# One decoder layer in fp32: the scheduler that orders each engine's instructions is given its other simulator

## The chip, the cores and the metric

The kernel runs on one core of one Trainium2 chip. The metric is the device time of one execution in microseconds (us); lower is better. Work is spread over TensorE (PE, matrix products; PEld is its weight load), VectorE (DVE), ScalarE (ACT), GpSimd (POOL) and the DMA queues, most of which are fed by SyncE (SP).

## What is computed

One layer of a hybrid decoder on 512 tokens of width 1024, all in fp32. The reference, cut to its frame:

```python
h = h + 0.5 * rmsnorm(swiglu(rmsnorm(h, ffn1_pre_w), ffn1_w_gu, ffn1_w_down), ffn1_post_w)
u = rmsnorm(h, mix_pre_w)
proj = u @ w_in                                    # 1024 x 10240, split into the branches' parts
y = gate0 * (hgrn2(...) @ w_br_hg) + gate1 * (dilated_attention(...) @ w_br_dil) \
  + gate2 * (memory_attention(...) @ w_br_mem)
h = h + rmsnorm(y @ w_out, mix_post_w)
h = h + 0.5 * rmsnorm(swiglu(rmsnorm(h, ffn2_pre_w), ffn2_w_gu, ffn2_w_down), ffn2_post_w)
```

`hgrn2` is a gated linear recurrence in chunks of 64 tokens, `dilated_attention` a sliding-window attention in three groups whose softmax statistics are merged, `memory_attention` a cross-attention into 256 memory tokens. `ffn1` and `ffn2` have 2816 hidden columns.

## The kernel before

**Products.** Every fp32 weight block is split into a high and a low part (`split`, L161 on ACT for the high part, L158 on DVE for the low part: lo = src - hi), so that three passes of a fast matmul replace one slow one: `mm3` (L341 to L343) for plain products, `product` (L361 to L363) for the Strassen-like products of `pair`, which computes two 128-row outputs from seven half-width products. The split parts live in a pool of 18 buffers named `w`; the raw weights arrive in 4 buffers `st`, 2 buffers `sh`, and 5 buffers `sum`. Where a pair needs sums of weight blocks, POOL starts DMAs that add while they copy (L303) or DVE adds (`sum<-...`). Activations stand in SBUF as `xhi`/`xlo` and `t1` to `t4`; PSUM has 5 buffers `ps` for the large products and 3 buffers `px` for everything smaller. A pool of 37 buffers `s` holds all other values.

**Stages.** FFN 1 runs to about 370 us, token mixing to about 1005 us, FFN 2 to the end. The seams between them are chains that go tile by tile (four tiles of 128 tokens): squares on ACT (L174), `rstd` with a sum on DVE (L180) and a power on POOL (L181), a scaling on DVE (L244 for the norm after a stage, L190 for the norm ahead of the next), transposes on PE (L352, `px<-ident,s`), and the split of the result (`xhi` on ACT, `xlo` on DVE). In token mixing, side tasks (HGRN heads, attention heads) issue small matmuls (L348, `px<-s,s`) between the large projections. A dilated head also exchanges its softmax statistics through DRAM: `x<-st` and then `ot<-x`, both DMAs of POOL's queue (L764 to L769), after which DVE merges them (`mm<-st,ot`).

**What sets the order.** Two things do. The source emits instructions in one sequence: a planner in the source (`spawn`, `tick`, the delays in `LAT`) decides where in the stream of large matmuls a side task's next step is emitted. This part is fixed text. Then the tile framework, when its context closes, runs a list scheduler: it plays the program on a simulated machine, and whenever a simulated engine is free it issues to it, of the instructions whose inputs and buffers are ready in the simulation, the one that stands first in the source's sequence. The order in which the simulated engine took them is the order in which the real engine gets them, and buffers of a pool are given out in that order too. The chip then runs each engine's list strictly from front to back, each instruction waiting on semaphores for its inputs. So an instruction that the simulation held ready too early stands too early in its list, and on the chip everything behind it on that engine waits with it.

**What is not free to move.** DMAs of `fetch` (L141) keep the source's order on SP; weight loads of `bring` (L151) may move among themselves behind an anchor. In the first stretch (`strict`, until FFN 1's first products start) `pin` also keeps splits, squares and DVE's two-operand work in the source's order.

## Time and profile before

| what | us |
|---|---|
| time, median of 3 runs (1366.94 to 1368.05) | 1367.82 |
| the profiled execution's own time | 1367.62 |
| its span, first to last instruction | 1365.8 |
| PE busy | 1331.6 |
| DVE busy | 1050.7 |
| ACT busy | 742.2 |
| POOL busy | 107.0 |

The granted TensorE clock was 0.998 of full speed on average over the span. Busy time of PE contains the pipelined tail of each matmul, so the idle time before an instruction is a little shorter than the time for which no matmul started. In views of the order of time a row gives the start, the length, the engine, the line, what is written from what, how many instructions were merged, and in brackets the idle time of that engine just before and what ended it.

### The profile page before, as it was taken

The numbers are of one execution on the slowest core, as the hardware profiler recorded it, in microseconds if no ns is written. First come the engines' busy times: TensorE is split into PE (matmuls) and PEld (weight loads), VectorE is DVE, ScalarE is ACT, GpSimd is POOL, SyncE is SP. The second block draws the span as 40 slices with busy tenths as digits, with TensorE's granted clock in tenths as the row PEclk, the third lists the DMA queues.
The fourth block names the chain that finished last, engine by engine and source line by source line (L and its number), as shares of the span: only waits on it lengthen the run. The fifth ranks groups of instructions, "written<-read, shape, count | busy, mean of one in ns | idle before, by whom it ended". The sixth has DMA issues, their size and how long they took to land.

```text
span 1365.8 us, 24324 instructions
## 1 busy us (share of the span) xinstructions
PE 1331.6 (97%) x9197; PEld 1233.0 (90%) x9197; DVE 1050.7 (77%) x1996; ACT 742.2 (54%) x1527; POOL 107.0 (8%) x140
## 2 busy tenths in 40 slices
PE   6999999999999999999999999999999999999997
PEld 6999999999789888899899999999889999999996
DVE  6887776777798975598888988897478877677765
ACT  6665544555467655355554755566366655445541
POOL 1111111110100000000000100000011111111100
PEclk9999999999999999999999999999999999999999
DMA  9676565554435335334224333335465765655513
GB/s 271 141 182 184 148 156 142 143 151 125 168 94 177 96 98 163 123 102 117 63 78 124 100 95 93 108 94 154 135 190 135 186 181 151 152 139 148 146 47 139
DMA packets 238123, 185.76 MB, mean 136 GB/s; under 512 B 9109, under 2 KB 198966, under 8 KB 238006
## 3 DMA queue, kind: packets, MB, share of 16 engines
q1 hardware_dynamic: 224246, 160.02, 39.5%
q0 software_dynamic: 12032, 21.04, 9.4%
q10 hardware_dynamic: 1728, 3.15, 0.6%
q8 instruction: 72, 1.18, 0.3%
q14 instruction: 45, 0.37, 0.1%
HBM read 153.73 MB, written 9.47 MB: 119 GB/s over the span
## 4 chain that ended last, share of the span: by engine, by line
PE 87%; DVE 6%; issue 3%; DMA 2%; ACT 1%; POOL 1%; SPq 0%; POOLq 0%; DVEq 0%; ACTq 0%
PE ps L361 17%; PE ps L363 17%; PE ps L362 17%; PE ps L341 6%; PE ps L342 6%; PE ps L343 6%; PE px L341 5%; PE px L342 5%; PE px L343 5%; PE px L348 4%; DVE s L158 2%; PE px L352 1%; DVE w L158 1%; POOL r L181 1%; DVE s L244 1%
## 5 line engine op out<-in xcount | busy, mean ns | idle before, releaser
L161 ACT ACTIVATE w<-sum 128x512 fp32r<-128x512 f32 x288 | 180.2, 631 | 215.9 <-PE ps L362 180.3
L158 DVE TENSOR_TENSOR w<-sum,w 128x512 fp32r<-128x512 f32 x288 | 196.9, 687 | 76.9 <-ACT w L161 75.9
L361 PE MATMUL ps<-xhi,w 128*128 128x256 f32 x864 | 246.3, 285 | 0.9 <-ACT s L379 0.9
L363 PE MATMUL ps<-xhi,w 128*128 128x256 f32 x864 | 244.8, 283 | 0.0
L362 PE MATMUL ps<-xlo,w 128*128 128x256 f32 x864 | 244.4, 283 | 0.0
L161 ACT ACTIVATE w<-st 128x512 fp32r<-128x512 f32 x260 | 162.9, 630 | 126.7 <-PE ps L362 90.0
L158 DVE TENSOR_TENSOR w<-st,w 128x512 fp32r<-128x512 f32 x260 | 177.2, 688 | 39.3 <-ACT w L161 37.9
L158 DVE TENSOR_TENSOR s<-s,s 128x256 f32<-128x256 f32 (+3 forms) x316 | 176.8, 564 | 16.2 <-ACT s L161 4.6
L361 PEld LDWEIGHTS ps<-xhi,w 128*128 128x128 f32 x864 | 165.6, 192 | 3.8 <-ACT s L379 1.2
L362 PEld LDWEIGHTS ps<-xlo,w 128*128 128x128 f32 x864 | 165.6, 192 | 2.4 <-issue 0.2
L363 PEld LDWEIGHTS ps<-xhi,w 128*128 128x128 f32 x864 | 165.5, 192 | 0.0
L158 DVE TENSOR_TENSOR sum<-sum,st 128x512 f32<-128x512 f32 x176 | 120.4, 687 | 10.9 <-issue 5.0
L158 DVE TENSOR_TENSOR s<-s,ps 128x256 f32<-128x256 f32 (+1 forms) x194 | 92.3, 476 | 29.4 <-PE ps L343 24.0
L341 PE MATMUL px<-s,s 128*128 128x512 f32 x288 | 112.6, 391 | 0.0
L342 PE MATMUL px<-s,s 128*128 128x512 f32 x288 | 112.5, 391 | 0.0
L343 PE MATMUL px<-s,s 128*128 128x512 f32 x288 | 112.0, 389 | 0.0
L361 PE MATMUL ps<-t4hi,w 128*128 128x256 f32 x288 | 81.9, 284 | 0.8 <-ACT s L382 0.8
L361 PE MATMUL ps<-t3hi,w 128*128 128x256 f32 x288 | 82.6, 287 | 0.0
L362 PE MATMUL ps<-t3lo,w 128*128 128x256 f32 x288 | 82.0, 285 | 0.0
L361 PE MATMUL ps<-t1hi,w 128*128 128x256 f32 x288 | 81.7, 284 | 0.0
L363 PE MATMUL ps<-t1hi,w 128*128 128x256 f32 x288 | 81.6, 283 | 0.0
L362 PE MATMUL ps<-t2lo,w 128*128 128x256 f32 x288 | 81.5, 283 | 0.0
(186 smaller groups left out, 3344.2 us busy)
## 6 DMA issues: line engine op xcount, KB each, us to landing
st<-in_ffn_w_gu_dram SPq DMA_DIRECT2D x48, 512.0 KB, 4.9
st<-in_w_in_dram SPq DMA_DIRECT2D x48, 512.0 KB, 3.7
st<-in_ffn_w_down_dram SPq DMA_DIRECT2D x44, 512.0 KB, 3.8
sum<-in_ffn_w_gu_dram SPq DMA_DIRECT2D x80, 256.0 KB, 3.4
sh<-in_ffn_w_gu_dram SPq DMA_DIRECT2D x40, 256.0 KB, 3.8
sum<-sh POOLq DMA_DIRECT2D x40, 256.0 KB, 3.6
sum<-st POOLq DMA_DIRECT2D x40, 256.0 KB, 3.3
sum<-in_w_in_dram SPq DMA_DIRECT2D x32, 256.0 KB, 2.9
```

Of the source, the lines that this page charges most:

```text
L158: self.pin(self.nc.vector.tensor_tensor(out=out, in0=a, in1=b, op=op))
L161: self.pin(self.nc.scalar.activation(hi, src, AF.Copy))
L181: self.nc.gpsimd.tensor_tensor(out=r, in0=v, in1=self.mhalf[:, :1], op=ALU.pow)
L244: self.nc.vector.scalar_tensor_tensor(out=h[hf][:, cs], in0=y[hf][:, cs], scalar=r, in1=h[hf][:, cs], op0=ALU.mult, op1=ALU.add)
L341: mm(out, lhsT=lhs[0], rhs=rhs[0], start=first, stop=False)
L342: mm(out, lhsT=lhs[0], rhs=rhs[1], start=False, stop=False)
L343: mm(out, lhsT=lhs[1], rhs=rhs[0], start=False, stop=last)
L348: self.nc.tensor.matmul(out, lhsT=lhsT, rhs=rhs, start=start, stop=stop, **k)
L352: self.nc.tensor.transpose(out, in_, self.ident)
L361: mm(out, lhsT=lh, rhs=rh, start=first and k == 0, stop=False, skip_group_check=True)
L362: mm(out, lhsT=lh, rhs=rl, start=False, stop=False, skip_group_check=True)
L363: mm(out, lhsT=ll, rhs=rh, start=False, stop=k == 3, skip_group_check=True)
```

## The change

One argument. The list scheduler plays the program on the framework's other simulator, which models queues and semaphores, instead of on its default one. The sequence that the source emits, the delays of its planner, all buffers and all instructions are as before; what can differ is each engine's order and which buffer a value gets.

```diff
     out = nc.dram_tensor("out_0_dram", _OUTS[0][0], _mybir.dt.float32, kind="ExternalOutput").ap()
-    with _tile.TileContext(nc) as tc:
+    with _tile.TileContext(nc, schedule_with_timeline_sim=True) as tc:
         layer_kernel(tc, args, nbias, hmask, out)
```

## Rows read from the trace of the kernel before

**Rows 1.** The page: busy us by engine (share of span, instructions).
```profile
span 1365.8 us, 24324 instructions
PE 1331.6 (97%) x9197; PEld 1233.0 (90%) x9197; DVE 1050.7 (77%) x1996; ACT 742.2 (54%) x1527; POOL 107.0 (8%) x140
```

**Rows 2.** Waits of PE, whole span: for whom, us in total, times, longest.
```profile
PE px L352 <- DVE s L190: 13.2, 5, 9.5
PE ps L342 <- DVE xlo L158: 3.2, 2, 1.9
PE px L348 <- DVE s L158: 2.2, 3, 1.0
PE ps L342 <- DVE w L158: 1.8, 1, 1.8
PE px L348 <- ACT s L585: 1.6, 1, 1.6
PE ps L361 <- ACT s L379: 0.9, 1, 0.9
PE ps L361 <- ACT s L382: 0.8, 1, 0.8
PE ps L341 <- ACT w L161: 0.7, 1, 0.7
PE ps L352 <- DVE s L190: 0.4, 1, 0.4
```

**Rows 3.** Waits of ACT with a weight split, same columns.
```profile
ACT w L161 <- PE ps L362: 289.1, 306, 4.9
```

**Rows 4.** PE in order of time around two side-task steps in token mixing.
```profile
456.72 0.63 PE L352 MATMUL px<-ident,s 128*128 128x128 f32 x4 [0.97 <-DVE s L190]
...
641.72 0.28 PE L362 MATMUL ps<-xlo,w 128*128 128x256 f32 x1
642.95 1.13 PE L348 MATMUL px<-s,s 128*128 128x128 f32 x8 [0.95 <-DVE s L158]
643.83 0.36 PE L363 MATMUL ps<-xhi,w 128*128 128x256 f32 x1
...
660.42 0.92 PE L348 MATMUL px<-s,s 128*128 128x256 f32 x3 [1.64 <-ACT s L585]
```

**Rows 5.** DVE in order of time where it merges a dilated head's statistics.
```profile
646.97 0.69 DVE L158 TENSOR_TENSOR w<-st,w 128x512 fp32r<-128x512 f32 x1
652.42 0.23 DVE L158 TENSOR_TENSOR mm<-st,ot 128x4 f32<-128x4 f32 x2 [4.76 <-DMA ot<-x]
```

**Rows 6.** POOL's queue in the same stretch.
```profile
649.53 0.76 POOL L768 DMA_DIRECT2D ot<-x  x1 [3.93 <-DMA x<-st]
```

**Rows 7.** Busy us by engine from 600 to 700 us: PE, PEld, DVE, ACT, POOL, clock, DMA.
```profile
600.00:700.00 100.00, 96.32 (x737) 90.25 (x737) 87.36 (x221) 54.07 (x144) 4.50 (x7) 1.00 0.32 88
```

**Rows 8.** ACT in order of time early in FFN 1.
```profile
65.88 0.63 ACT L161 ACTIVATE w<-sum 128x512 fp32r<-128x512 f32 x1 [1.58 <-DVE sum L158]
66.41 0.35 ACT L382 COPY s<-ps 128x256 f32<-128x256 f32 x1
```

**Rows 9.** DVE in order of time at the seam of FFN 1 and mixing.
```profile
378.91 1.54 DVE L244 SCALAR_TENSOR_TENSOR s<-s,r,s 128x512 f32<-128x512 f32 x3 [0.44 <-POOL r L181]
380.37 0.68 DVE L158 TENSOR_TENSOR w<-st,w 128x512 fp32r<-128x512 f32 x1
```

**Rows 10.** PE at the two seams.
```profile
381.11 0.50 PE L342 MATMUL ps<-w,xhi 128*128 128x512 f32 x1 [1.78 <-DVE w L158]
...
1008.33 0.39 PE L342 MATMUL ps<-xlo,w 128*128 128x256 f32 x1 [1.92 <-DVE xlo L158]
```

**Rows 11.** Waits of DVE on POOL's power, whole span: us in total, times, longest.
```profile
DVE s L190 <- POOL r L181: 5.7, 11, 0.7
DVE s L244 <- POOL r L181: 5.0, 10, 0.7
```

**Rows 12.** ACT in order of time around two loads of its function table.
```profile
151.65 1.28 ACT L841 ACT_TABLE_LOAD   x1
152.95 0.21 ACT L841 ACTIVATE pcols<-pcols 128x8 f32<-128x8 f32 x1
153.17 1.28 ACT L431 ACT_TABLE_LOAD   x1
```

## The prediction, made before the changed kernel was run

> **What bounds the kernel now.** I read the busy line of the page first: PE is busy for 1331.6 of 1365.8 us, DVE for 1050.7, ACT for 742.2 [rows 1]. Matmuls are the same before and after, so their 1331.6 us stay; an order can only win or lose idle time of PE, 1365.8 - 1331.6 = 34.2 us. The table of PE's waits says what that time is [rows 2]. Its rows add up to 24.8 us. The remaining 9.4 us (34.2 - 24.8) belong to no wait of PE: the end of the span, where the last tile is normed and stored. Of the 24.8 us the longest wait, 9.5, is the one before the first transpose. Two more belong to the first stretch, whose DVE and ACT work is pinned: the 0.4 us on L352 into `ps`, and 3.2 - 1.9 = 1.3 us on `xlo`. That leaves 24.8 - 9.5 - 1.7 = 13.6 us in 13 waits, 1.05 us each, on which the scheduler has a say. PE never waits for a transfer in that table, and in the FFNs it is ACT that waits for PE to free a weight buffer, 306 times for 289.1 us [rows 3]: splits run as far ahead as the 18 buffers allow. So most of the span gives no PE time to win, and a shift of a microsecond on ACT or DVE is hidden there.
>
> I sort the 13.6 us into four groups.
> - **A, side tasks in mixing, 4.8 us:** 2.2 and 1.6 us at L348 [rows 2] and 0.97 us at 456.72 [rows 4].
> - **B, copies out of PSUM early in FFN 1, 1.7 us:** L379 and L382 [rows 2].
> - **C, the two seams, 6.4 us:** 13.2 - 9.5 - 0.97 = 2.7 us at transposes, 1.9 us on `xlo` and 1.8 us on a weight split [rows 2, 10].
> - **D, one wait on a weight's high part, 0.7 us** [rows 2].
>
> **Why the present order has them.** PE at 641.72 is in the middle of a group of projection matmuls, goes to L348 and idles 0.95 us for DVE; the next matmul of the same group starts right behind it, at 643.83 [rows 4]. That matmul needed nothing from DVE. A list scheduler that had seen DVE late would have issued the group's rest first. So the simulation had DVE done before the chip does, and the same shape stands at 456.72. The clearest case is the exchange of statistics through DRAM: DVE's list has the merge at a place where the chip waits 4.76 us for `ot` [rows 5], because POOL could issue that transfer only at 649.53, after 3.93 us of waiting for the first hop [rows 6]. DVE's other work stood behind the merge all that time, in a stage where DVE is busy 87% [rows 7], and the 1.64 us of PE at 660.42 [rows 4] come soon behind. In group B ACT sat 1.58 us before a weight split whose sum DVE had not finished, and the copy that PE waits for stood behind that split [rows 8].
>
> **The change part by part.** No instruction of the source is added or removed. What the trace of before can't show is the new order itself, so each group is bounded from both sides.
>
> A: a simulation with queues and semaphores should hold DVE, ACT and the exchange ready later, which puts the px work later in PE's list, behind matmuls that are ready. Between 0 and 4.8 us are to be had; I take four fifths, **-3.8**, because the matmul that could go first is in the rows. The cover is the projection behind it; where it is gone, the wait stays.
>
> B: between 0 and 1.7 us. Only L382's wait has a queue order as its cause in the rows, so **-0.8**.
>
> C: at 378.91 DVE idled 0.44 us for POOL's power, then scaled, and only then did the weight subtraction that PE wanted, at 380.37 for 0.68 us [rows 9]; PE resumed at 381.11 [rows 10]. With POOL's time known, the subtraction goes into the gap: 378.47 + 0.68 = 379.15, which is 1.9 us sooner and covers the 1.78 us. I take 1.3 of it, and the same 1.3 for the wait at 1008.33 by analogy: **-2.6** (bounds 0 and -3.7). Of the 2.7 us at transposes I take half, **-1.4**: other matmuls can fill in, but the next stage hangs on these transposes.
>
> The price of C: each such filling makes the norm chain late. The gap is 0.44 us and the filler 0.68, so 0.24 us a time. DVE waits for POOL 21 times, 10.7 us in all [rows 11]; 16 of these are in the two seams (four tiles, two norms, two seams). 16 x 0.24 = 3.8 us; PE has the previous stage's matmuls to do at the first tiles of a seam, so I charge half, **+1.9**. Bounds: 0 (no filler ready) to 16 x 0.68 = 10.9 us (each filler begins just before the power lands).
>
> D: one wait, no cause in the rows: 0 (bounds -0.7 and +0.7).
>
> New waits: the other simulator errs too, in other places. The present one leaves 13 waits of 1.05 us; I charge two, **+2.1** (bounds 0 and 13 of them, 13.6). The first stretch and the end I leave at 0: the former is pinned, and at the end hardly any other work is left to be put in front of the last tile's chain; a filler of 0.68 us there would count in full. Weight loads on SP can change places among themselves. That costs nothing while splits are so far ahead [rows 3]; if that cover were lost, a wait like the 1.78 us at 381.11 [rows 10] is the nearest price, and it is inside the bound for new waits.
>
> **Sum:** -3.8 - 0.8 - 2.6 - 1.4 + 1.9 + 2.1 = -4.6 us. The profiled execution took 1367.62 us, so 1363.0; the median of the runs lies 0.2 us above it, so **1363.2**.
>
> **Rivals.**
> 1. *The waits only move.* The sequence that the source emits is fixed, PE mostly follows it, and new misjudgments cost what the old ones did, or the lists come out nearly as they are. For it: the planner's delays are fixed numbers that keep most px work far from its inputs' end, so few places react. Against it: the 4.76 us wait shows an order that the chip's own times contradict [rows 5]. Time: 1367.8, give or take 2.7.
> 2. *Slower: fillers in the norm chains.* A simulation that shows a gap at each hop between ACT, DVE and POOL puts a ready 0.68 us subtraction into each, just before the hop lands. Place: the two seams, where the next stage hangs on the chain. Price: 10.9 us in place of 1.9, so -4.6 + 9.0 = +4.4 and 1372.2. It decides once the slip per gap passes s with 16 s = 3.8 + 0.8 + 2.6 + 1.4 - 2.1 = 6.5, that is 0.41 us. For it: in these seams the weight splits of the next stage are ready work [rows 9]. Against it: the gaps are mostly known to be shorter than a filler, and early tiles have cover.
> 3. *Slower: ACT changes its function table more often.* A table load takes 1.28 us each [rows 12]. Side tasks use exponentials, logarithms and sigmoids; an order that interleaves them more finely loads more often. Six more loads in mixing, if they hit work that PE waits for like L585, are 6 x 1.28 = 7.7 us, so 1363.2 + 7.7 = 1370.9. Against it: ACT is busy 54% [rows 1], so most loads would be hidden. This is the rule that speaks against the change: the Trainium skill, "ScalarE: Activation LUTs", section "What ACT_TABLE_LOAD costs", puts a switch of tables at 1283 ns of load and some 1380 ns of drain, 2.66 us together, and would make the six loads about 16 us, an estimate from that page. The trace agrees with the load and shows no drain behind it: the function that follows starts at 152.95, when the load that began at 151.65 has just ended [rows 12].
> 4. *Faster by much.* All 13.6 us go and no wait comes: 1367.8 - 13.6 = 1354.2. It would take a simulation without error.
>
> **How the numbers follow.** About 0.2% (2.7 us) is what a measurement of this kernel can tell from no change. Chances: the forecast 0.40, rival 1 0.24, rival 2 0.20, rival 3 0.08, rival 4 0.08. Faster by over 0.2%: 0.40 + 0.08 = 0.48; within: 0.24; slower: 0.28. The forecast's own range is 1359 to 1365. The range for 8 in 10 must reach across rivals 1 to 3 with some room for more new waits (three more than in rival 2, 1372.2 + 3.2 = 1375.4) and below nearly to rival 4: 1355 to 1375.
>
> **What would show it.** Right: PE's waits at L348 shrink from 3.8 us to under 1; DVE's 4.76 us wait for `ot` is gone or short; weight subtractions stand in DVE's 0.44 us gaps at the seams; PE's busy time is unchanged within a few us; table loads stay near 14. Wrong: px work still idles PE in the midst of a projection group; the seams' last tile comes later by several us; PE waits for weights or for a transfer in the middle of a stage; many more table loads than 14.

## The result, and the profile after

| what | before | after |
|---|---|---|
| time, median of 10 runs each, same chip | 1367.53 us | 1374.69 us |
| ratio, 95% interval | | 1.0050 [1.0039, 1.0061] |
| the profiled execution's own time | 1367.62 | 1373.49 |
| its span | 1365.8 | 1371.7 |

The changed kernel is slower by half a per cent. Some 7 us were lost where 4.6 were forecast as a gain. The sign was wrong; the time lies just inside the range. The two profiled executions, on which the rest is read, lie 5.9 us apart.

The page of the changed kernel, as in [rows 1]:

```profile
span 1371.7 us, 24387 instructions
PE 1334.5 (97%) x9197; PEld 1236.9 (90%) x9197; DVE 1054.6 (77%) x1996; ACT 744.4 (54%) x1527; POOL 107.2 (8%) x140
```

The instructions of each engine are as many as before. PE's busy time grew by 2.9 us and its idle time by 3.0 (37.2 against 34.2). Both have to be explained: the same matmuls are busy longer only if they run slower.

PE's waits, whole span: for whom, us in total, times, longest.

```profile
PE px L352 <- DVE s L190: 9.1, 1, 9.1
PE px L352 <- DVE s L589: 4.4, 1, 4.4
PE ps L341 <- ACT xhi L161: 3.6, 4, 1.7
PE ps L341 <- ACT s L450: 3.4, 2, 2.3
PE ps L342 <- DVE xlo L158: 2.5, 1, 2.5
PE ps L361 <- ACT s L860: 2.4, 1, 2.4
PE ps L361 <- ACT s L372: 1.5, 1, 1.5
```

Against [rows 2], all waits at L348 are gone, and so are the four other transposes' waits for L190 and the wait for a weight's low part. New are single long ones: 4.4 us for the memory head's normalization (L589), 2.5 on `xlo`, 2.4 on L860, 2.3 on L450. Behind the first stretch, thirteen waits of 1.05 us on average became eleven of 1.6.

To see where the time went, I laid the two traces side by side at equal matmul work: every matmul counts with its step at full clock (0.12 us for 256 columns, 0.23 for 512), and the table compares the moments at which the two kernels reached the same sum. It is worked out from all matmul rows of the two traces; the lists differ, so a moment inside a stage can be off by some tenths.

```
before at   after - before    what lies in between
  46.7 us       -0.3 us       start
  93.9          -2.3          first pairs of FFN 1 (group B)
 364.4          -2.6          rest of FFN 1
 399.5          -4.8          first seam
 476.1          -2.2          L860's wait of 2.36 at 453.06
 662.8          -7.5          side tasks (group A)
 678.4          -2.3          L589's wait of 4.40 at 664.53, slow clock
 739.4          -1.3          L372's wait of 1.53 at 697.27
 995.9          -0.6          rest of mixing
1013.6          +3.8          second seam, first half
1029.6          +7.3          second seam, second half
1356.5          +7.3          FFN 2
   end          +5.9          last tile
```

So the gains that the forecast named were made, in their places. Besides L860's wait (2.6 us), two places gave more back: 6.2 us of mixing right behind the side tasks' gain, and 7.9 us in the second seam.

**Mixing.** PE in order of time after the last scores of the memory head (L348):

```profile
659.10 1.03 PE L348 MATMUL px<-s,s 128*128 128x256 f32 x4
664.53 1.94 PE L352 MATMUL px<-ident,s 128*128 128x128 f32 x8 [4.40 <-DVE s L589]
...
666.48 0.41 PE L362 MATMUL ps<-xlo,w 128*128 128x256 f32 x1
666.69 0.41 PE L363 MATMUL ps<-xhi,w 128*128 128x256 f32 x1
...
667.58 0.28 PE L362 MATMUL ps<-xlo,w 128*128 128x256 f32 x1
667.70 0.28 PE L363 MATMUL ps<-xhi,w 128*128 128x256 f32 x1
```

The same stretch in the kernel before:

```profile
661.21 0.47 PE L361 MATMUL ps<-xhi,w 128*128 128x256 f32 x1
...
666.07 1.04 PE L352 MATMUL px<-ident,s 128*128 128x128 f32 x8
```

Before, 4.9 us of projection matmuls stand between the last scores and the first transposes, from 661.21 to 666.07. After, nothing stands in between. Those matmuls went ahead of the scores, where they removed the 2.2 and 1.6 us of waits at L348 [rows 2]. The cover was spent earlier.

That is one half. Two memory heads run here side by side, and the transposes at 664.53 belong to the first of them, while the scores at 659.10 belong to the second: the first head's sum of exponentials is inverted on DVE (L586) at 662.88, and the exponentials of the last scores start only after that, at 662.92. So PE waits for the first head's softmax, whose steps on DVE are maxima of the scores (L581), their scaling (L582), the inversion (L586) and the normalization (L589). DVE after:

```profile
653.24 0.68 DVE L581 TENSOR_REDUCE mmx<-px 128x2 f32<-128x512 f32 x1
...
654.44 1.29 DVE L158 TENSOR_TENSOR w<-sum,w 128x512 fp32r<-128x512 f32 x2
...
657.13 0.17 DVE L582 TENSOR_SCALAR mnm<-mmx 128x2 f32<-128x2 f32 x1
...
662.88 0.15 DVE L586 RECIPROCAL ml<-ml 128x4 f32<-128x4 f32 x1
...
664.02 1.14 DVE L589 TENSOR_SCALAR s<-s,ml 128x256 f32<-128x256 f32 x4
```

and before:

```profile
658.35 0.69 DVE L581 TENSOR_REDUCE mmx<-px 128x2 f32<-128x512 f32 x1
...
662.20 1.14 DVE L589 TENSOR_SCALAR s<-s,ml 128x256 f32<-128x256 f32 x4
```

From the first maximum to the first normalization it is 3.9 us before and 10.8 after. Before, no sum or subtraction of weights stands in between; after, eleven do, of 0.6 us each, some 6.6 us in all. The other half of the wait is DVE's list.

On PE, the last four rows after show the clock's part of the price: matmuls of the same shape start 0.21 us apart at 666.48 and 0.12 apart at 667.58.

**Second seam.** Busy us by engine (PE, PEld, DVE, ACT, POOL), clock, DMA, after:

```profile
1010.00:1015.00 5.00, 4.12 (x19) 4.13 (x20) 3.95 (x8) 3.17 (x9) 1.43 (x2) 0.50 1.05 283
...
1000.00:1035.00 35.00, 28.38 (x181) 26.27 (x180) 26.84 (x48) 21.94 (x48) 5.43 (x7) 0.85 0.42 121
```

and before:

```profile
1000.00:1035.00 35.00, 32.22 (x244) 30.36 (x243) 32.02 (x59) 25.14 (x55) 5.41 (x7) 1.00 0.39 113
```

In these 35 us PE starts 181 matmuls instead of 244, at a mean clock of 0.85 instead of 1.00. PE around the second tile's transposes (L352), after:

```profile
1004.45 0.60 PE L352 MATMUL px<-ident,s 128*128 128x128 f32 x4
1004.81 0.48 PE L343 MATMUL ps<-w,s 128*128 128x512 f32 x1
1005.13 0.60 PE L352 MATMUL px<-ident,s 128*128 128x128 f32 x4
1007.43 0.91 PE L341 MATMUL ps<-xhi,w 128*128 128x256 f32 x4 [1.71 <-ACT xhi L161]
1010.88 0.58 PE L342 MATMUL ps<-xlo,w 128*128 128x256 f32 x1 [2.54 <-DVE xlo L158]
...
1028.91 0.39 PE L341 MATMUL ps<-xhi,w 128*128 128x256 f32 x1 [2.32 <-ACT s L450]
```

and before:

```profile
1002.51 1.03 PE L352 MATMUL px<-ident,s 128*128 128x128 f32 x8
1003.30 0.47 PE L341 MATMUL ps<-w,s 128*128 128x512 f32 x1
...
1005.90 0.40 PE L343 MATMUL ps<-w,s 128*128 128x512 f32 x1
1006.13 0.28 PE L341 MATMUL ps<-xhi,w 128*128 128x256 f32 x1
```

Here it is the cover. Before, twelve matmuls of mixing's last product stand behind these transposes, from 1003.30 to 1006.13, while ACT and DVE split the result. After, one is left, and PE waits 1.71 and then 2.54 us. The split itself takes about as long in either kernel: the last transpose starts at 1003.27 before and 1005.45 after, the first product with `xlo` 5.1 and 5.4 us later.

The norm chain of the last two tiles is late as well. DVE after:

```profile
1004.56 1.89 DVE L158 TENSOR_TENSOR w<-st,w 128x512 fp32r<-128x512 f32 x3
...
1008.81 1.42 DVE L244 SCALAR_TENSOR_TENSOR s<-s,r,s 128x512 f32<-128x512 f32 x2 [0.44 <-POOL r L181]
...
1015.93 1.41 DVE L190 SCALAR_TENSOR_TENSOR s<-s,r,s 128x512 f32<-128x512 f32 x2 [1.98 <-POOL r L181]
```

and before:

```profile
1010.04 1.41 DVE L190 SCALAR_TENSOR_TENSOR s<-s,r,s 128x512 f32<-128x512 f32 x2 [0.45 <-POOL r L181]
```

The third tile's L190 comes 5.9 us later. On the way the chain stands behind three weight subtractions in a row on DVE (1004.56), behind a weight split on ACT that waits for its load, and on POOL behind a DMA that adds:

```profile
1011.42 0.63 ACT L161 ACTIVATE w<-st 128x512 fp32r<-128x512 f32 x1 [1.05 <-DMA st<-in_ffn_w_gu_dram]
1011.96 0.62 ACT L174 ACTIVATE s<-s 128x512 f32<-128x512 f32 x1
...
1027.18 1.28 ACT L450 ACT_TABLE_LOAD   x1
```

```profile
1014.46 0.85 POOL L303 DMA_DIRECT2D sum<-st  x1 [1.88 <-ACT s L174]
1015.02 0.88 POOL L181 TENSOR_TENSOR r<-v,mhalf 128x1 f32<-128x1 f32 x1
```

### The profile page after: what moved, and what is told of

Same layout as the page of the kernel before. It is cut to its first block, busy times and chain, and to the rows that moved or that the text cites. A ratio compares the mean times of both kernels' runs of the same rounds, so it can differ in the third digit from the quotient of the medians.

```text
span 1371.7 us, 24387 instructions
## 1 busy us (share of the span) xinstructions
PE 1334.5 (97%) x9197; PEld 1236.9 (90%) x9197; DVE 1054.6 (77%) x1996; ACT 744.4 (54%) x1527; POOL 107.2 (8%) x140
## 4 chain that ended last, share of the span: by engine, by line
PE 93%; DVE 2%; ACT 2%; DMA 1%; issue 1%; SPq 0%; POOL 0%; DVEq 0%; POOLq 0%; ACTq 0%
PE ps L361 18%; PE ps L362 17%; PE ps L363 17%; PE ps L341 7%; PE ps L342 7%; PE ps L343 7%; PE px L342 5%; PE px L341 5%; PE px L343 5%; PE px L348 4%; PE px L352 1%; DMA s<-in_x_dram 1%; DVE w L158 1%; DMA st<-in_ffn_w_gu_dram 1%; ACT s L174 0%
## 5 line engine op out<-in xcount | busy, mean ns | idle before, releaser
L158 DVE TENSOR_TENSOR w<-sum,w 128x512 fp32r<-128x512 f32 x288 | 197.6, 689 | 68.9 <-ACT w L161 67.5
L158 DVE TENSOR_TENSOR w<-st,w 128x512 fp32r<-128x512 f32 x260 | 177.2, 690 | 40.4 <-ACT w L161 33.7
L158 DVE TENSOR_TENSOR s<-s,s 128x256 f32<-128x256 f32 (+3 forms) x316 | 176.8, 565 | 12.0 <-ACT s L161 3.0
L158 DVE TENSOR_TENSOR s<-s,ps 128x256 f32<-128x256 f32 (+1 forms) x194 | 92.9, 480 | 55.2 <-PE ps L363 38.4
L158 DVE TENSOR_TENSOR sum<-sum,st 128x512 f32<-128x512 f32 x176 | 119.3, 686 | 5.4 <-issue 2.7
L361 PE MATMUL ps<-t1hi,w 128*128 128x256 f32 x288 | 82.2, 286 | 0.0
L362 PE MATMUL ps<-t1lo,w 128*128 128x256 f32 x288 | 82.1, 285 | 0.0
```

What stands on the lines that cost most here:

```text
L158: self.pin(self.nc.vector.tensor_tensor(out=out, in0=a, in1=b, op=op))
L361: mm(out, lhsT=lh, rhs=rh, start=first and k == 0, stop=False, skip_group_check=True)
L362: mm(out, lhsT=lh, rhs=rl, start=False, stop=False, skip_group_check=True)
```

## The experiments

Most experiments put the old order of some engines back for one stretch. A few lines behind the source's end add edges of pure issue order between the listed instructions, each to the one ahead of it. The data and the waits for inputs stay. The scheduler plays the program anew around these edges, so all that is not listed can come out in an order that is neither kernel's (the code is shortened):

```diff
         layer_kernel(tc, args, nbias, hmask, out)
+        graft(tc, GRAFT)
...
+def graft(tc, runs):
+    at = {i.name: i for i in tc.nc.cur_bb.bb.instructions}
+    for run in runs:                     # one run: instruction numbers in the order wanted
+        seq = [f"I-{n}" for n in run.split()]
+        for a, b in zip(seq, seq[1:]):
+            tc.add_manual_dep(at[b], a, NoSync, reason="graft")
```

Each ratio below is to the kernel before on the same chip in the same session, so ratios are compared with each other rather than medians. The changed kernel's own is 1.0050. Expected times stand on the scale of 1367.8 us for the kernel before; where it matters, a ratio is put on that scale.

### Is the second seam the place, and the order there the cause?

`s2_all`: the changed kernel, with the order of before on PE, DVE, ACT and POOL between 985 and 1036 us.

```diff
+GRAFT = [ 321 of PE, 72 of DVE, 54 of ACT, 10 of POOL ]   # 985 to 1036 us
```

> The changed kernel, but in the second seam (985 to 1036 us) PE, DVE, ACT and POOL get the order of the kernel before among the instructions that they ran there. The comparison of the two traces puts 7.9 us of the loss into this seam. If the orders in the seam are the cause: 1366.8 us (1374.7 - 7.9), and no fall of the granted clock there. Rival, that the seam is late because of what comes before it (buffers given out in another order, weights that arrive later): 1373 to 1375.

Measured: 1369.78 us, 1.0015 [1.0002, 1.0027], or 1369.9 on the scale of the expectation: between the two theories. In the trace the seam costs 0.9 us instead of 7.9, and the clock does not fall in it:

```profile
1000.00:1035.00 35.00, 31.88 (x236) 29.35 (x236) 31.47 (x58) 25.41 (x57) 5.46 (x7) 1.00 0.42 121
```

By the ratios 0.35% comes back, that is 4.8 us. The profiled execution (1367.33 us) is one of the two fastest of ten, which reach up to 1372.67; its mean clock was 0.997, that of six of the other nine 0.995 or lower. So the trace shows more than the median gives. Shown is that the order on these four engines in these 50 us is the place and the cause of most of the 7.9 us; whether the remaining 3 come into the seam from elsewhere stays open.

### Which engine's list is it?

`s2_dve`, `s2_pool`, `s2_act` and `s2_pe` take one of the four lists each, `s2_dap` takes the three without PE.

```diff
-GRAFT = [ 321 of PE, 72 of DVE, 54 of ACT, 10 of POOL ]
+GRAFT = [ 72 of DVE ]        # s2_dve;   s2_pool: 10 of POOL;  s2_act: 54 of ACT
+GRAFT = [ 321 of PE ]        # s2_pe
+GRAFT = [ 72 of DVE, 54 of ACT, 10 of POOL ]   # s2_dap
```

> As s2_all, but the order of before is given back on DVE alone. Theory 1, DVE's fillers in front of the norm chain are the cause: at least 5 of the 7.9 us come back, 1367 to 1370. Theory 2, POOL's weight adds in front of the power, or theory 3, ACT waiting for a load in front of the squares: under 2.5 us come back, 1372 to 1375.

> As s2_all, but on POOL alone: two weight adds go back behind two of the powers; the other engines' lists stay as in the changed kernel. Theory 2: DVE's wait of 1.98 us for the power shrinks to 0.73 or less, and PE gets back 1.3 us and what the lower clock costs on top, 1371 to 1373. Theories 1 and 3: under 0.7 us, 1374 to 1375.

> As s2_all, but the order of before is given back on ACT alone. Theory 3, ACT's list is the cause (a weight split that waits for its load stands in front of a square, and splits of w in front of splits of xhi): at least 4 of the 7.9 us come back, 1368 to 1371. Theory 5, no single engine's list is the cause but the four together: under 2 us, 1373 to 1375.

> As s2_all, but on PE alone. Theory 4, PE's own list is the cause (the simulation found it idle and pulled matmuls forward, so that the last products ahead of the seam come late): at least 4 us come back, 1368 to 1371. Theory 5: under 2 us, 1373 to 1375.

> The changed kernel with the old order on DVE, ACT and POOL, but not on PE, between 985 and 1036 us. All four together gave back 4.9 us of the changed kernel's 1374.7, PE alone 1.6, DVE alone 0.7. Theory P (the norm chain is on these three engines, and PE's list only follows it): 1369.5 to 1371, the second seam within 1.5 us of before. Theory F (the four lists fit only each other): 1372.5 to 1375, the seam costs 4 us or more, with a wait of PE over 2 us in it.

| old order on | time | ratio, 95% | what the seam costs in its trace |
|---|---|---|---|
| DVE | 1373.97 | 1.0047 [1.0029, 1.0064] | 6.2 us |
| POOL | 1375.35 | 1.0054 [1.0039, 1.0069] | 6.9 |
| ACT | 1376.71 | 1.0058 [1.0040, 1.0075] | 7.1 |
| PE | 1373.05 | 1.0035 [1.0022, 1.0047] | 5.9 |
| DVE, ACT and POOL | 1375.36 | 1.0036 [1.0023, 1.0048] | 6.2 |
| all four | 1369.78 | 1.0015 [1.0002, 1.0027] | 0.9 |

No single list put back carries it, and neither do the three of the chain. But only `s2_pool` differs from the changed kernel in one list alone. Laid row by row against the changed kernel, `s2_pe` has 57 of DVE's 1996 instructions at another place, from 1002 to 1058 us, `s2_dve` has 554 of PE's 9197, up to 1136 us, `s2_act` 525 of PE's and `s2_dap` 520. And two of the grafts lose more behind their end, which the table leaves out: between 1050 and 1100 us `s2_act` loses 4.5 us (a wait of 2.94 for L466 at 1067.28) and `s2_dve` 3.0 (1.70 for L158 at 1074.38). So the rows below show where each mixture waits; what one list is worth with all others as in the changed kernel is measured for POOL only. With PE's old list alone the cover behind the second tile's transposes is back, and PE then runs into the late chain of the third tile:

```profile
1016.15 1.94 PE L352 MATMUL px<-ident,s 128*128 128x128 f32 x8 [4.18 <-DVE s L190]
```

With the chain's three old lists alone, the transposes still stand behind the whole of mixing's last product:

```profile
1008.02 1.03 PE L352 MATMUL px<-ident,s 128*128 128x128 f32 x8
...
1012.87 0.39 PE L342 MATMUL ps<-xlo,w 128*128 128x256 f32 x1 [1.88 <-DVE xlo L158]
```

As far as these mixtures tell, two things are wrong at once, spent cover on PE and a late chain, and either alone is enough to lose some 6 us. Among the single lists the order by size is not to be read; their intervals overlap.

### What is L589's wait in mixing?

`a_mem14` makes the source's planner emit the memory head's transposes later; `a_lean` leaves out the weight sums for the second pair of dilated heads (about 14 us of DVE's work; an unsummed block takes their place, so this kernel does not compute the layer); `m_dve` and `m_all` put the old order back between 625 and 690 us, on DVE alone and on all four engines.

```diff
-LAT = dict(comb=1.0, mem0=0.5, mem1=8.0, mem2=1.5, ...
+LAT = dict(comb=1.0, mem0=0.5, mem1=14.0, mem2=1.5, ...     # a_mem14
...
-    def wops(self, w, c1, c2, by_load):
+    def wops(self, w, c1, c2, by_load, lean=False):           # a_lean
...
+            if lean:
+                return sums["a21"]
...
+GRAFT = [ 150 of DVE ]                                  # m_dve
+GRAFT = [ 407 of PE, 150 of DVE, 76 of ACT, 6 of POOL ] # m_all
```

> The changed kernel with the planner's delay between a memory head's scores and its transposes raised from 8 to 14 us, so that the transposes for which PE waits 4.4 us at 664.53 stand behind more projection matmuls. Theory A, only the place in PE's list is wrong: 4.5 us and the half clock behind it come back, 1368 to 1370. Theory B, DVE has no room in this stretch, so that PE would then wait for DVE somewhere else within 30 us: under 1.5 us come back, 1373 to 1375.

1374.51, 1.0046 [1.0030, 1.0063]. The wait for L589 is gone, and PE waits at the same place for something else:

```profile
666.76 0.58 PE L361 MATMUL ps<-xhi,w 128*128 128x256 f32 x1 [5.33 <-ACT s L372]
```

```profile
666.24 0.20 ACT L585 ACTIVATION_READ_ACCUMULATOR s<-px,mnm 128x1 f32 x1
666.34 0.37 ACT L372 COPY s<-ps 128x256 f32<-128x256 f32 x1
```

The next product needs a result copied out of PSUM (L372), and that copy stands on ACT directly behind the memory head's exponentials (L585). So the transposes' place on PE was not the cause: with the projection matmuls already spent, PE has nothing ready here, whichever of the two stands first. DVE's part of the first head's softmax takes 10.8 us here too (654.51 to 665.30), with the same eleven weight operations in it. The Trainium skill, "PSUM — Partial Sum Buffer", section "Engine vs sequencer instructions", says that ScalarE's queue is strictly first in, first out. The rows agree: the copy's result was waited for during 5.33 us, and the copy started when the exponentials had ended.

> The changed kernel without the weight sums that DVE makes for the second pair of dilated heads (24 additions of 0.60 us less, 14 us of DVE work between about 645 and 770 us; products use an unsummed block). Theory B, DVE has no room there: PE's waits of 4.4 us at 664.53 and 1.5 us at 697.27 shrink to under 2 us together and 4 to 6 us come back, 1369 to 1371. Rival, the waits are the length of a chain: they stay, 1373.5 to 1375.

1376.16, 1.0047 [1.0031, 1.0064]. The wait stays, 4.73 us at 666.74, and DVE, with less to do, waited 3.84 us for `ot` at 653.32 instead. Its part of the softmax still takes 9.6 us (656.64 to 666.25), with six weight operations and other work between the steps. Less work on DVE does not remove the wait as long as what is left stands between those steps.

> The changed kernel with before's DVE order among the instructions of 625 to 690 us. Theory C, the weight sums that the new list puts ahead of the memory head's work on DVE cause PE's 4.4 us at 664.53: the wait shrinks under 2 us and 2 to 4 us come back, 1371 to 1373. Theory B, DVE has no room in this stretch whatever its order: PE waits as long, there or nearby, 1374 to 1376.

1376.82, 1.0058 [1.0036, 1.0081]. The wait shrank to 1.14 us at 661.22 plus 1.01 behind it, as theory C has it: DVE's part of the softmax is down to 4.7 us (656.01 to 660.73), without a weight operation in it. From 628 to 690 us this kernel gains 2.7 us on the kernel before, where the changed kernel loses 0.6, and the waits at L348 do not come back (0.4 and 0.2 us are left). All of it is lost right behind the stretch, 7.3 us between 690 and 700, at the transposes of the next pair of heads:

```profile
689.20 0.68 DVE L581 TENSOR_REDUCE mmx<-px 128x2 f32<-128x512 f32 x1
...
697.35 1.13 DVE L589 TENSOR_SCALAR s<-s,ml 128x256 f32<-128x256 f32 x4
697.84 1.94 PE L352 MATMUL px<-ident,s 128*128 128x128 f32 x8 [3.84 <-ACT s L585]
```

It is the same fault at another place: nine weight operations stand between that pair's first maximum and its first normalization, which takes 8.2 us; before and after it takes 3.9 and 4.3. That part of DVE's list is not in the graft, and it is neither kernel's. PE's and ACT's lists are not quite the changed kernel's either (283 and 107 places differ, from 637 to 729 us). So the time of this run does not decide on theory C; the waits speak for it, in both places.

> The changed kernel with the old order on PE, DVE, ACT and POOL between 625 and 690 us. Theory G (the gain at the side tasks and the wait of 4.40 us at 664.53 belong to one order: whoever gives up the one gives up the other): 1374 to 1376, no wait of PE over 2 us between 650 and 700, and PE's waits of before at L348 back. Theory L (the waits at 664.53 and 697 are a loss of their own, that the old order doesn't have and that brings nothing): 1369 to 1371.5.

1371.87, 1.0014 [1.0000, 1.0027]; on the scale of the expectation 1369.7. PE's waits there are those of before again:

```profile
PE px L348 <- DVE s L158: 1.8, 2, 1.0
PE px L348 <- ACT s L585: 1.6, 1, 1.6
```

No wait over 2 us is left between 650 and 700 us, and DVE's part of the softmax takes 4.7 us (657.44 to 662.10). The time is theory L's, the waits are theory G's. By the ratios the old order here is worth 0.36%, 4.9 us; the trace shows only about 1 of them as matmul progress (from 628 to 739 us the changed kernel loses 1.6 against before, `m_all` 0.6). But the clock of `m_all` fell to 0.50 from 659.7 to 663.1, behind the wait of 1.65 us at L348, which in the kernel before, at 1.64 us, had left it at 1.00; 1.6 us of progress were lost there. The profiled execution was also 1.5 us above its median. So the trace undersells the old order. What is shown: with the old order of all four engines the 3.4 us at L348 come back and the 4.40 + 1.53 us go, and this is the better of the two. Its size stays open between 1 and 5 us. That the one gain can't be had without the other loss is not shown; `m_dve` had both up to 690 us.

### Do the gains hold by themselves?

`b_s1` is the kernel before with the new order only where the table of progress showed gains; `best1` and `best2` are the changed kernel with the old order where it showed losses.

```diff
+GRAFT = [ new order of all four engines in 50 to 100 and 335 to 405 us ]               # b_s1, on the kernel before
+GRAFT = [ old order of all four engines in 430 to 810 and 985 to 1036 us ]             # best1
+GRAFT = [ old order of all four engines in 0 to 50, 430 to 810 and 985 to 1036 us ]    # best2
```

> The kernel before, with the old scheduler, but with the changed kernel's order on PE, DVE, ACT and POOL in two stretches alone, 50 to 100 us (the two ACT copies) and 335 to 405 us (the first seam). The comparison of the traces has the changed kernel 2.1 us and 2.5 us ahead there. If these gains belong to the orders there: 1363 to 1364, against 1367.8. Rival, that they are owed to what came before: 1366.5 to 1368.

1370.25, 1.0014 [1.0000, 1.0028], slower than both theories have it. The seam gave 1.6 us, but a wait of 2.60 us for L372 came at 64.19, the clock fell behind it, and 0.8 and 1.5 us were lost at 411.88 and 724.77. The new order of FFN 1's start does not gain inside the old lists.

> The changed kernel with before's order on PE, DVE, ACT and POOL in token mixing (430 to 810 us) and in the second seam (985 to 1036 us). If gains and losses belong to the stretches in which they show: the 4.8 us that the changed kernel is ahead at 420 us stay, and the two stretches cost what they cost before, 1363 to 1365. Rival, that lists grafted in one stretch do not fit the buffers and the other lists around it: 1367 to 1370.

1366.56, 0.9982 [0.9971, 0.9992]; on the scale of the expectation 1365.3. This one is faster than both kernels, by 0.18% against before.

> The changed kernel with the old order on all four engines in 0 to 50, 430 to 810 and 985 to 1036 us, so that the new order is left in the FFNs and the first seam. With 430 to 810 and 985 to 1036 alone it was 1366.6, and 2.7 us were lost in its start. If the new order is what costs them: 1364 to 1365. If the start only differs from run to run: 1366 to 1367.

1367.39, 0.9985 [0.9973, 0.9998]. The old order in the first 50 us brings nothing, so the 2.7 us that `best1` lost in its start do not come from the new order there; the changed kernel, with that order, was 0.3 us ahead at the same place. The two versions agree within their intervals: the new order in the FFNs and the first seam is worth 0.15 to 0.18%, some 2 us.

The shares add up within their intervals of some 0.13% each: -0.35% for the seam and -0.36% for mixing, from 1.0050, are 0.9979, and `best1` measures 0.9982. It is not quite the same sum, since `best1` has the old order from 430 to 810 us (the 2.6 us at L860 included) and `m_all` from 625 to 690.

### Is one engine's list good by itself?

`a_pe` and `a_dve` give the changed kernel one whole list of before.

```diff
+GRAFT = [ all of PE, in the order of before ]    # a_pe
+GRAFT = [ all of DVE, in the order of before ]   # a_dve
```

> The changed kernel's scheduler, but PE's list is before's over the whole span. If the loss comes from PE's list (matmuls pulled forward while the simulated PE idled): 1367 to 1370. If it comes from the lists of DVE and ACT, or from all together: 1373 to 1377.

> As a_pe, but with DVE's list of before over the whole span and the new scheduler's lists elsewhere. If DVE's list carries the loss (rival 2 of the prediction): 1367 to 1370, with the second seam as before. If not: 1373 to 1377.

1393.79, 1.0170 [1.0146, 1.0195], and 1389.53, 1.0149 [1.0124, 1.0174]. `a_pe` waits 5.67 us at 790.76 for L372 and 4.12 at 1037.19. Both are outside what either theory had. The other engines' lists are not the changed kernel's here: the scheduler made them anew around the given one, and with `a_pe` at least 725 of DVE's 1996 instructions stand at another place than in the changed kernel. One list imposed on this scheduler from outside costs three times what the change costs.

## Why the prediction was wrong

| step | forecast | measured in the traces |
|---|---|---|
| A, side tasks | -3.8 | -5.3 by 663 us, then +6.2 by 739 |
| B, copies early in FFN 1 | -0.8 | -2.0 |
| C, first seam | half of -2.1 | -2.2 |
| C, second seam | half of -2.1 | +7.9 |
| new waits | +2.1 | the +6.2 above, +2.6 at L860, and part of the +7.9 |
| start, end | 0 | -0.3, -1.4 |

**Right.** The bound (PE's idle time), the diagnosis of [rows 4] and [rows 5], and groups A and B as places of gain. The waits at L348 vanished, DVE's 4.76 us for `ot` too (the merge stands at 648.72 without a wait), and PE resumed earlier in the first seam. There the gain did not come through DVE's gaps, though: its last weight subtraction in that seam starts at 369.95, ahead of the norm chain, and the gaps behind it stay open (0.44 to 0.73 us). Table loads are 14 in both kernels, so rival 3 did not come about. One of them became visible all the same: the load at 1027.18 lies inside PE's 2.32 us wait for L450, while before it began at 1021.08 and was covered.

**Wrong, step A.** "I take four fifths, because the matmul that could go first is in the rows. The cover is the projection behind it; where it is gone, the wait stays." The matmul did go first. What I did not ask is what else the new lists would put there. The same projection had later covered 4.9 us between the last scores and the first transposes, and DVE's new list put eleven weight operations into the first head's softmax, 10.8 us in place of 3.9. A gain made by pulling ready work forward has to be booked against the next place where that work was the cover, and against the chain that it now stands in. The term of -3.8 stood alone; behind it the traces show +6.2, in which are the waits of 4.40 and 1.53 us and the half clock from 663.9 to 667.3.

**Wrong, step C for the second seam.** "And the same 1.3 for the wait at 1008.33 by analogy." The first seam's wait was for a weight split behind a scaling, and an order could cure it [rows 9]. The second seam's wait of 1.92 us was for `xlo` [rows 10], the chain's own end, which no filler shortens; and the new order spent mixing's last matmuls before the transposes. The analogy was the error: the one wait was on ready work in the wrong place, the other on the critical chain.

**Wrong, the size of new waits.** I charged two of 1.05 us, the size of the old ones. The seven largest new ones behind the first stretch are 1.0 to 4.4 us, 15.9 us together (4.40, 2.54, 2.36, 2.32, 1.71, 1.53, 1.00). The largest stands at the end of a chain of several steps, the softmax with DVE's other work in between, and not at a single step.

**Rival 2** named the place and the side, with 1372.2, but not the mechanism. DVE's waits for POOL's power are 6.0 + 4.6 = 10.6 us after, 10.7 before [rows 11], and in the second seam there are seven in either kernel, 3.6 us before and 6.0 after; these gaps were not filled. (The rows have seven such gaps in each seam, 14 and not the 16 that the price of C and rival 2 count.) The weight work went in blocks ahead of a step of the chain (1.89 us at 1004.56), on ACT and POOL as well, and with DVE's old order put back only 1.7 of the seam's 7.9 us come back. That the range holds the time at all is owed to this rival and the three more waits added to it, and so to luck: the loss came another way.

**Not foreseen at all:** the clock. In the seam it costs about 3.7 of the 7.9 us, if nothing else would have held PE there. From 1010.88 to 1015.52 PE starts 21 matmuls of 256 columns in 4.64 us where they would take 21 x 0.12 = 2.52; from 1028.91 to 1032.66 it is 18 in 3.75 against 2.16. Matmuls that last 0.41 us instead of 0.28 are also what made PE's busy time grow.

**Open.** Why the other simulator's order pulls these matmuls forward and puts weight work into the softmax was not tried; only the resulting order was. Open too are the size of the loss in mixing, as said with `m_all`, the wait at L860, which no run takes by itself, and what each list of the second seam is worth alone.

## What to carry to other kernels

A scheduler that fills an early gap takes its filler from somewhere and puts it in front of something: before counting a gain, look for the wait that this work covers later, above all at the ends of chains (softmax to transposes, norm to the next stage), and for the chain that the filler now delays. To find the latter, follow one chain on the engine that is not the bottleneck, from its first step to its last, in both kernels; here that showed 3.9 against 10.8 us. An order that is forced on one engine makes the scheduler choose the others anew, so compare all lists before reading a result: in the seam no list alone gave back more than about a quarter in the trace (2.0 of 7.9 us), four together nearly all (7.0 in the trace, 4.8 by the ratios), and a whole list forced on the other scheduler cost 1.5 to 1.7%. Where two whole orders win in different stages, take each stage's lists from the kernel that wins it; here this gave 0.18% below the better one.

## What the runs showed of the hardware

The granted TensorE clock fell to half after waits of PE that are short beside the stage: 0.50 from 663.9 to 667.3, around the end of the wait of 4.40 us, from 1008.7 to 1015.5 around those of 1.71 and 2.54, and from 1029.2 to 1032.6 behind 2.32. The length of the wait alone does not decide. The changed kernel's 2.36 us at 453.06 left the clock at 1.00, as it did in `s2_all`, `s2_dap` and `a_mem14`; the same 2.36 us at 453.93 in `m_all` was followed by 0.50 from 454.9 to 458.3 (and the like in `s2_act`, `s2_pool`, `s2_dve`, `s2_pe`, `m_dve` and `a_lean`). A wait of 1.65 us was followed by 0.50 in `m_all` (659.7 to 663.1), one of 1.64 [rows 4] and the 1.92 us of [rows 10] were not. The rows show only two cadences for 256 columns, 0.21 us and 0.12 us from start to start. The Trainium skill, "TensorE: Matmul & The Clock Gate", section "What's actually happening", knows two levels, 1.2 and 2.4 GHz; by them 256 columns would take 0.213 and 0.107 us, an estimate from that page, and the rows agree with the first and lie 0.01 above the second.
